# A 64-column bf16 product that nobody reads, in front of four weight blocks of every up stage and of the gated unit's output product

## The chip, the cores and the metric

The kernel runs on one core of a Trainium2 chip. The time is device microseconds of that core for one launch, from inputs in HBM to the output in HBM. The kernel before took 1655.77 us, the median of three runs (1654.12 to 1661.84). The profiled execution took 1660.22 us, of which 1658.4 us is the span from the first to the last instruction.

## The reference

Two blocks of transformer layers over one sequence of 256 tokens with model width 1024, all in float32. What matters here are the six feed-forward networks (two with a short convolution, four plain SwiGLU) and the gated unit (gMLP) between them; the two attention mixers and the linear recurrence lie around them.

```python
def conv_ffn(x, w_up, conv_w, conv_b, w_down):          # twice, D_FF = 2816
    h = x @ w_up                                        # (256,1024) @ (1024,5632)
    h = depthwise_causal_conv3(h, conv_w) + conv_b
    gate, up = split(h, 2)
    return (silu(gate) * up) @ w_down

def swiglu(n, w_gate, w_up, w_down):                    # four times
    return (silu(n @ w_gate) * (n @ w_up)) @ w_down

def gmlp_mixer(n, w_in, ln_g, ln_b, w_s, b_s, w_out):   # once
    u, v = split(gelu(n @ w_in), 2)
    sv = causal_mix_of_positions(w_s, layer_norm(v, ln_g, ln_b)) + b_s
    return (u * sv) @ w_out                             # (256,2048) @ (2048,1024)
```

Every network takes `rms_norm` of the running sum h, and its result is added to h (in the second block after another `rms_norm`).

## The kernel before, in words

All products run in float32 accuracy from three products of a faster float32 form: activations and weights are each split into a high part and a rest (hi, lo), and xh*wh, xl*wh and xh*wl are added up in PSUM. So TensorE does three products of 256 columns for each 128x128 tile of weights.

A weight block is 1024 rows by 256 columns (1 MB). `fetch` brings it from HBM by SyncE's DMA queue into one of three `wst` buffers; `unit` (L228) splits it: ScalarE writes `whi` (L249), VectorE writes `wlo` (L251), in four pieces for the first blocks of a stage and whole afterwards, into four buffers each. `feat2` (L267) then computes 256 output features for all 256 tokens: two halves of 24 products (`feat`, L261 to L265), 48 in all, into one of four PSUM buffers `acc`. `tok` (L280 to L291) is the same with the tokens as rows.

An up stage has 11 passes, i = 0 to 10, with two blocks each (gate and up columns). In `conv_ffn` (L663) every pass uses `feat2`. In `swiglu` (L626) passes 1 to 10 use `feat2`, and pass 0 does, in the last three of the four networks, something else (L635 to L653): the norm's factor comes late, so both blocks are computed token half by token half with `tok_turn`; ScalarE applies silu to each half (L645), VectorE multiplies (L646, result `ffu`), and TensorE turns `ffu` back to feature rows by four transposes (L650), two for each token half, into the PSUM buffer `turned`. Before them `p.finish()` (L647) broadcasts the factor with two products (L370); in the network beside which the shared keys are prepared it also transposes h for them, in four groups of four (L412), each into one of two PSUM buffers `mx`, which ScalarE and VectorE (L306, L308) must have emptied before.

After the 11 passes `down` (L545) multiplies the hidden features by the down weights (L565 to L567, and L576 to L578 for its last quarter or half), and at its quarters h is updated and transposed for the next norm (L400, L412).

I call the networks by their order: conv 1, conv 2, SwiGLU 1 to 4. SwiGLU 2 follows the gated unit; SwiGLU 3 carries the shared keys; SwiGLU 4 ends the program. SwiGLU 2, 3 and 4 have the special pass 0.

The order on each engine is fixed when the program is built: a scheduler runs through the program with a time model and lays down each engine's queue. It may let a product that is written later overtake an earlier one that is not ready. `behind()` (L192) forbids that: what is issued within it stands behind the instruction that was written last on TensorE. Each engine takes its queue strictly in order.

Of the kernel before, what the change touches and what calls it, by code (L numbers as in the profile page):

```python
# [15 lines left out]
P = 128  # L16
D = 1024
T = 256
KD = 8
# [35 lines left out]
MLA_ORDER = "N0 V0 N1 V1 V2 P0 P1 Q0 R0 Q1 R1 S0 Q2 S1 T0 Q3 O0 S2 T1 S3 V3 O1 T2 O2 T3 O3"  # L55
TURN_OLD, TURN_NEW = (8, 5), (6, 4)
N_HOLD = 3
N_START = 12
L_MLA = 2
RSQRT_BITS = float(0x5F375A86)  # L60
# [87 lines left out]
class Net:  # L148
# [48 lines left out]
    def warm(s, n):  # L197

        if n:
            with s.behind():  # L200
                ps = s.prod()
                x = s.ident.bitcast(BF16)
                for _ in range(n):
                    s.nc.tensor.matmul(ps[:, :T], x[:, :P], x, start=True, stop=True)


    def fetch(s, parts, k0, nk, cuts=1):

# [55 lines left out]
            mm(ps, wh[:, k, cols], xl, start=False, stop=False)  # L264
            mm(ps, wl[:, k, cols], xh, start=False, stop=k == nk - 1)  # L265

    def feat2(s, w, x, c=0, beside=None):  # L267

        ps = s.acc()
        s.parts(lambda j: s.feat(w, c + j, x, ps[:, j * T:(j + 1) * T]), beside)  # L270
        return ps

# [202 lines left out]
    def start(s, first):  # L475
# [29 lines left out]
        p = s.pre(s.vec("attn_norm"))  # L505
        s.warm(N_START)
        for n in range(4):
# [37 lines left out]
    def down(s, w, hid, kn, out, n_beside=0):  # L545
# [36 lines left out]
        for n in range(4 - out.late, 4):  # L582
            ps = [s.acc()[:, :T], s.acc()[:, :T]]
            for i, (k0, nk) in enumerate(spans):
                u = s.unit([(w, n * T, T)], k0, nk)
                for t in range(2):
                    if len(spans) - i > N_HOLD:
                        part(ps[t], t, u, k0)
# [37 lines left out]
    def swiglu(s, p, wg, wu, wd, out, beside=None):  # L626
        nc = s.nc
        hid = Split(s, "f", KF)
        s.begin(p)
        for i in range(KF // 2):  # L630
            if beside and i == 3:
                beside()
            g, u = s.e("ffg"), s.m("ffu")
            h2 = lambda x: x.rearrange("p (j t) -> p j t", j=2)
            if p.halves and i == 0:  # L635

                units = [s.unit([(m, 0, T)], 0, KD) for m in (wg, wu)]
                turned = s.mix()
                for t in range(2):
                    c, ps, r = slice(t * T, (t + 1) * T), s.acc(), p.r[:, t:t + 1]  # L640
                    s.tok_turn(p, units, t, ps, () if t else TURN_NEW)
                    if not t:
                        last = p.marks[-1][0]
                    with s.tc.issue_after(last):
                        nc.scalar.activation(g[:, c], ps[:, :T], AF.Silu, scale=r)  # L645
                    nc.vector.scalar_tensor_tensor(u[:, c], ps[:, T:], r, g[:, c], op0=OP.mult, op1=OP.mult)  # L646
                p.finish()  # L647
                for t in range(2):
                    for j in range(2):
                        nc.tensor.transpose(turned[:, j * T + t * P:j * T + (t + 1) * P],  # L650
                                            u[:, t * T + j * P:t * T + (j + 1) * P], s.ident)
                s.split(hid.hi.pair(0), hid.lo.pair(0), turned)
                continue  # L653
            ps = s.feat2(s.unit([(wg, i * T, T)], 0, KD), p.x)
            nc.vector.tensor_tensor(h2(g), h2(ps), s.rb2(p), op=OP.mult)
            nc.scalar.activation(g, g, AF.Silu)
            ps = s.feat2(s.unit([(wu, i * T, T)], 0, KD), p.x)
            nc.vector.tensor_tensor(h2(u), h2(ps), s.rb2(p), op=OP.mult)  # L658
            nc.vector.tensor_tensor(u, u, g, op=OP.mult)
            s.split(hid.hi.pair(i), hid.lo.pair(i), u)  # L660
        s.down(wd, hid, KF, out)

    def conv_ffn(s, p, l, out):  # L663
        nc, a = s.nc, s.a
        w = a["ffn_w_up"][l]
        hid = Split(s, "f", KF)
        s.begin(p)

        def conv(y, x, c):
            taps = [s.vec("conv_w%d%d" % (i, l), c, 1) for i in range(3)]  # L670
            nc.scalar.activation(y, x, AF.Identity, scale=taps[2], bias=s.vec("conv_b%d" % l, c, 1))
            nc.vector.scalar_tensor_tensor(y[:, 1:], x[:, :T - 1], taps[1], y[:, 1:], op0=OP.mult, op1=OP.add)
            nc.vector.scalar_tensor_tensor(y[:, 2:], x[:, :T - 2], taps[0], y[:, 2:], op0=OP.mult, op1=OP.add)

        h2 = lambda x: x.rearrange("p (j t) -> p j t", j=2)
        for i in range(KF // 2):
            if l == 0 and i in (3, 6):

                if i == 3:
                    turns = s.conv_vectors(1)  # L680
                else:
                    with s.behind():
                        for turn in turns:
                            turn()
            ys = [s.e("cvg"), s.m("cvu")]
            for y, first in zip(ys, (0, KF)):
                c = first + 2 * i
                ps = s.feat2(s.unit([(w, c * P, T)], 0, KD), p.x)
                x = s.z("cvx")
                nc.vector.tensor_tensor(h2(x), h2(ps), s.rb2(p), op=OP.mult)  # L690
                for j in range(2):
                    half = slice(j * T, (j + 1) * T)
                    conv(y[:, half], x[:, half], c + j)
                if not first:
                    nc.scalar.activation(y, y, AF.Silu)
            g, u = ys
            nc.vector.tensor_tensor(u, u, g, op=OP.mult)
            s.split(hid.hi.pair(i), hid.lo.pair(i), u)
        s.down(a["ffn_w_down"][l], hid, KF, out)
# [690 lines left out]
    def gmlp(s, p, out):  # L1390
        nc, a = s.nc, s.a
        V, S, PE = nc.vector, nc.scalar, nc.tensor
        w = a["gmlp_w_in_2"][0]
# [5 lines left out]
        for c in range(4):  # L1399
            units = [s.unit([(w, half + (2 * c + j) * T, T)], 0, KD) for j in range(2)]  # L1400
            for t in range(2):
# [7 lines left out]
                ps = s.acc()  # L1409
# [19 lines left out]
        for c in range(8):  # L1429
            ps = s.feat2(s.unit([(w, c * T, T)], 0, KD), p.x)  # L1430
            x, y = s.e("gx"), s.m("gy")
            V.tensor_tensor(h2(x), h2(ps), s.rb2(p), op=OP.mult)
            S.activation(x, x, AF.Gelu_apprx_tanh)
            sp = s.prod()
            for j in range(2):
                g = 2 * c + j
                cols = slice((g % 4) * P, (g % 4 + 1) * P)
                for n in range(2):
                    i = 2 * j + n
                    PE.matmul(sp[:, i * P:(i + 1) * P], v[n][g // 4][:, cols], wt[g // 4][:, cols],  # L1440
                              start=True, stop=True)
            for j in range(2):
                g = 2 * c + j
                cols = slice((g % 4) * P, (g % 4 + 1) * P)
                hf = slice(j * T, (j + 1) * T)
                V.scalar_tensor_tensor(h2(y[:, hf]), h2(sp[:, hf]), ln_g[:, g:g + 1],
                                       radd[g // 4][:, cols][:, None, :].to_broadcast([P, 2, P]),
                                       op0=OP.mult, op1=OP.add)
            V.tensor_tensor(y, y, x, op=OP.mult)
            s.split(z.hi.pair(c), z.lo.pair(c), y)  # L1450
        s.down(a["gmlp_w_out_2"][0], z, 16, out)

    def rope_tables(s):
# [322 lines left out]
```

## Time and profile before

| | |
|---|---|
| Median of three runs | 1655.77 us (1654.12 to 1661.84) |
| Profiled execution | 1660.22 us, span 1658.4 us |
| TensorE products (PE) | busy 1622.1 us, 98% of the span, 14500 of them |
| VectorE (DVE) | busy 1150.2 us, 69% |
| ScalarE (ACT) | busy 913.1 us, 55% |
| HBM | 291.19 MB read, 178 GB/s over the span |

A busy time is a union of intervals, and products overlap in it, so 98% does not say that TensorE runs as fast as it can: for that one counts products in a stretch. PEclk in the views is the granted TensorE clock, 1.00 being 2.4 GHz and 0.50 being 1.2 GHz. PEld is the loading of the weights of a product.

### The profile page before, as it was taken

The numbers are of one execution on the slowest core, as the hardware profiler recorded it, in microseconds if no ns is written. First come the engines' busy times: TensorE is split into PE (matmuls) and PEld (weight loads), VectorE is DVE, ScalarE is ACT, GpSimd is POOL, SyncE is SP. The second block draws the span as 40 slices with busy tenths as digits, with TensorE's granted clock in tenths as the row PEclk, the third lists the DMA queues.
The fourth block names the chain that finished last, engine by engine and source line by source line (L and its number), as shares of the span: only waits on it lengthen the run. The fifth ranks groups of instructions, "written<-read, shape, count | busy, mean of one in ns | idle before, by whom it ended". The sixth has DMA issues, their size and how long they took to land.

```text
span 1658.4 us, 34159 instructions
## 1 busy us (share of the span) xinstructions
PE 1622.1 (98%) x14500; PEld 1608.4 (97%) x14502; DVE 1150.2 (69%) x1900; ACT 913.1 (55%) x1443; POOL 6.7 (0%) x28
## 2 busy tenths in 40 slices
PE   8989999996999999999999999999999999999998
PEld 8979999995999999999999999999999999999998
DVE  6997899545769975766668757664676647576643
ACT  7876665443666555544466446444664448574442
POOL 0000000000000000000000000000000000000000
PEclk9999999997999999999999999999999999999999
DMA  8733655677546556556756556556475665446551
GB/s 266 220 97 114 200 178 188 191 141 177 157 149 208 173 181 216 182 186 217 231 161 211 168 175 197 186 169 206 130 233 189 193 201 151 132 153 212 189 190 58
DMA packets 303821, 297.58 MB, mean 179 GB/s; under 512 B 14295, under 2 KB 300214, under 8 KB 303670
## 3 DMA queue, kind: packets, MB, share of 16 engines
q1 hardware_dynamic: 303622, 295.40, 57.4%
q8 instruction: 114, 1.87, 0.5%
q14 instruction: 37, 0.30, 0.1%
q10 hardware_dynamic: 48, 0.01, 0.0%
HBM read 291.19 MB, written 4.19 MB: 178 GB/s over the span
## 4 chain that ended last, share of the span: by engine, by line
PE 88%; DVE 4%; DMA 3%; ACT 3%; issue 1%; SPq 0%; DVEq 0%; ACTq 0%
PE acc L263 16%; PE acc L265 16%; PE acc L264 16%; PE acc L565 8%; PE acc L567 7%; PE acc L566 7%; PE acc L289 2%; PE acc L290 2%; PE acc L291 2%; DMA bias_rows<-rrow 2%; PE acc L576 2%; PE acc L578 2%; PE acc L577 2%; DVE wlo L251 1%; ACT whi L249 1%
## 5 line engine op out<-in xcount | busy, mean ns | idle before, releaser
L249 ACT ACTIVATE whi<-wst 128x2048 fp32r<-128x2048 f32 (+4 forms) x404 | 523.8, 1330 | 517.5 <-issue 228.6
L251 DVE TENSOR_TENSOR wlo<-wst,whi 128x2048 fp32r<-128x2048 f32 (+4 forms) x404 | 621.0, 1561 | 251.6 <-ACT whi L249 249.6
L264 PE MATMUL acc<-xl,whi 128*128 128x256 f32 x2416 | 675.2, 280 | 1.1 <-DVE xl L308 1.1
L263 PE MATMUL acc<-xh,whi 128*128 128x256 f32 x2416 | 675.3, 281 | 0.8 <-ACT xh L306 0.4
L265 PE MATMUL acc<-xh,wlo 128*128 128x256 f32 x2416 | 674.7, 280 | 0.5 <-DVE wlo L251 0.5
L264 PEld LDWEIGHTS acc<-xl,whi 128*128 128x128 f32 x2416 | 458.1, 190 | 1.7 <-DVE xl L308 1.5
L265 PEld LDWEIGHTS acc<-xh,wlo 128*128 128x128 f32 x2416 | 455.0, 189 | 0.9 <-DVE wlo L251 0.7
L263 PEld LDWEIGHTS acc<-xh,whi 128*128 128x128 f32 x2416 | 454.3, 188 | 1.6 <-ACT xh L306 0.7
L567 PE MATMUL acc<-wlo,fh 128*128 128x256 f32 x880 | 245.3, 279 | 0.0
L565 PE MATMUL acc<-whi,fh 128*128 128x256 f32 x880 | 244.7, 279 | 0.0
L566 PE MATMUL acc<-whi,fl 128*128 128x256 f32 x880 | 244.5, 278 | 0.0
L567 PEld LDWEIGHTS acc<-wlo,fh 128*128 128x128 f32 x880 | 165.2, 188 | 0.0
L565 PEld LDWEIGHTS acc<-whi,fh 128*128 128x128 f32 x880 | 165.0, 188 | 0.0
L566 PEld LDWEIGHTS acc<-whi,fl 128*128 128x128 f32 x880 | 164.9, 187 | 0.0
L289 PE MATMUL acc<-whi,xh 128*128 128x256 f32 x384 | 108.9, 284 | 0.0
L291 PE MATMUL acc<-wlo,xh 128*128 128x256 f32 x384 | 106.8, 278 | 0.0
L290 PE MATMUL acc<-whi,xl 128*128 128x256 f32 x384 | 106.8, 278 | 0.0
L289 PEld LDWEIGHTS acc<-whi,xh 128*128 128x128 f32 x384 | 72.1, 188 | 0.2
L290 PEld LDWEIGHTS acc<-whi,xl 128*128 128x128 f32 x384 | 72.1, 188 | 0.0
L291 PEld LDWEIGHTS acc<-wlo,xh 128*128 128x128 f32 x384 | 72.1, 188 | 0.0
L658 DVE TENSOR_TENSOR ffu<-acc,rb 128x512 f32<-128x512 f32 x41 | 28.3, 691 | 48.5 <-PE acc L265 48.3
L308 DVE SCALAR_TENSOR_TENSOR xl<-mx,vectors,xh 128x128 fp32r<-128x128 f32 (+1 forms) x124 | 39.1, 376 | 23.1 <-ACT xh L306 23.0
(422 smaller groups left out, 2097.3 us busy)
## 6 DMA issues: line engine op xcount, KB each, us to landing
wst<-in_ffn_w_up_dram SPq DMA_DIRECT2D x88, 1024.0 KB, 5.2
wst<-in_ffn_w_down_dram SPq DMA_DIRECT2D x48, 1024.0 KB, 5.9
wst<-in_ffn_w_gate_dram SPq DMA_DIRECT2D x44, 1024.0 KB, 5.4
wst<-in_ffn_w_down_dram SPq DMA_DIRECT2D x24, 768.0 KB, 4.8
wst<-in_gmlp_w_in_dram SPq DMA_DIRECT2D x16, 1024.0 KB, 5.4
wst<-in_hgrn_w_in_dram SPq DMA_DIRECT2D x13, 1024.0 KB, 5.5
wst<-in_gmlp_w_out_dram SPq DMA_DIRECT2D x8, 1024.0 KB
wst<-in_dsa_w_in_dram SPq DMA_DIRECT2D x6, 1024.0 KB
```

Source lines behind the costliest of these rows:

```text
L249: s.nc.scalar.activation(hi[:, c], w[:, c], AF.Copy)
L251: s.nc.vector.tensor_tensor(lo[:, c], w[:, c], hi[:, c].bitcast(F32), op=OP.subtract)
L263: mm(ps, wh[:, k, cols], xh, start=k == 0, stop=False)
L264: mm(ps, wh[:, k, cols], xl, start=False, stop=False)
L265: mm(ps, wl[:, k, cols], xh, start=False, stop=k == nk - 1)
L289: mm(ps, xh[:, ts], wk, start=k == 0, stop=False)
L290: mm(ps, xl[:, ts], wk, start=False, stop=False)
L291: mm(ps, xh[:, ts], lk, start=False, stop=k == nk - 1)
L308: b = s.nc.vector.scalar_tensor_tensor(lo, src, g, hi.bitcast(F32), op0=OP.mult, op1=OP.subtract)
L565: mm(ps[t], xh, wh[:, k], start=k0 + k == 0 and not both, stop=False)
L566: mm(ps[t], xl, wh[:, k], start=False, stop=False)
L567: mm(ps[t], xh, wl[:, k], start=False, stop=k0 + k == kn - 1 and (t == 1 or not both))
```

## The change

`pace` issues one product of the bf16 identity matrix with 64 of its own columns into a `pr` buffer in PSUM, behind whatever was written before it. Nobody reads the result. With `paced=True`, `feat2` issues such a product first, puts the first half of its 24 products behind it, and then the second half. It is on for passes i = 1 and i = 2 of all six up stages, two blocks each, and one `pace` stands in front of the gated unit's `down`: 25 products in all.

```diff
+PACED = (1, 2)
...
+    def pace(s):
+
+        with s.behind():
+            s.nc.tensor.matmul(s.prod()[:, :64], s.identb, s.identb[:, :64], start=True, stop=True)
...
-    def feat2(s, w, x, c=0, beside=None):
+    def feat2(s, w, x, c=0, beside=None, paced=False):

         ps = s.acc()
+        if paced:
+            s.pace()
+            with s.behind():
+                s.feat(w, c, x, ps[:, :T])
+            s.feat(w, c + 1, x, ps[:, T:])
+            return ps
         s.parts(lambda j: s.feat(w, c + j, x, ps[:, j * T:(j + 1) * T]), beside)
         return ps
...
-            ps = s.feat2(s.unit([(wg, i * T, T)], 0, KD), p.x)
+            ps = s.feat2(s.unit([(wg, i * T, T)], 0, KD), p.x, paced=i in PACED)
             nc.vector.tensor_tensor(h2(g), h2(ps), s.rb2(p), op=OP.mult)
             nc.scalar.activation(g, g, AF.Silu)
-            ps = s.feat2(s.unit([(wu, i * T, T)], 0, KD), p.x)
+            ps = s.feat2(s.unit([(wu, i * T, T)], 0, KD), p.x, paced=i in PACED)
...
-                ps = s.feat2(s.unit([(w, c * P, T)], 0, KD), p.x)
+                ps = s.feat2(s.unit([(w, c * P, T)], 0, KD), p.x, paced=i in PACED)
...
+        s.pace()
         s.down(a["gmlp_w_out_2"][0], z, 16, out)
```

The line numbers move by up to 14: L263 to L265 become L270 to L272, L289 to L291 become L302 to L304, L370 becomes L383, L412 becomes L425, L650 becomes L663; the new product is L211.

The queue of TensorE at the end of pass 0 of SwiGLU 2, before (L291 ends pass 0, `ffu` is the turned input of L650, `pr` the factor's broadcast, L263 begins pass 1):

```order
L291 MATMUL acc<-wlo,xh 128x256
L650 MATMUL mx<-cst,ffu 128x128 x2
L370 MATMUL pr<-cst,pr 128x128
L263 MATMUL acc<-xh,whi 128x256
...
L650 MATMUL mx<-cst,ffu 128x128 x2
L264 MATMUL acc<-xl,whi 128x256
```

The second pair of transposes stands 70 products behind the start of pass 1. The same place now:

```order
L304 MATMUL acc<-wlo,xh 128x256
L663 MATMUL mx<-cst,ffu 128x128 x2
L383 MATMUL pr<-cst,pr 128x128
L663 MATMUL mx<-cst,ffu 128x128 x2
L211 LDWEIGHTS identb
L211 MATMUL pr<-identb 128x64
L270 MATMUL acc<-xh,whi 128x256
```

Both pairs now stand in front of the new product and so in front of all of pass 1; in SwiGLU 4 the rows move in the same way, by 70 products.

The queue of TensorE at the same place of SwiGLU 3, before (L412 are the groups of transposes of h for the shared keys):

```order
L291 MATMUL acc<-wlo,xh 128x256
L370 MATMUL pr<-cst,pr 128x128
L412 MATMUL mx<-cst,h 128x128 x4
L263 MATMUL acc<-xh,whi 128x256
...
L412 MATMUL mx<-cst,h 128x128 x4
...
L412 MATMUL mx<-cst,h 128x128 x4
...
L650 MATMUL mx<-cst,ffu 128x128 x4
```

The second group stands 14 products, the third 79 and the four transposes of `ffu` 84 products behind the start of pass 1. Now:

```order
L304 MATMUL acc<-wlo,xh 128x256
L383 MATMUL pr<-cst,pr 128x128
L425 MATMUL mx<-cst,h 128x128 x12
L663 MATMUL mx<-cst,ffu 128x128 x4
L211 LDWEIGHTS identb
L211 MATMUL pr<-identb 128x64
L270 MATMUL acc<-xh,whi 128x256
```

All three groups and the four transposes stand in front of pass 1.

## Rows read from the trace of the kernel before

**Rows 1.** The page: busy time by engine, and the chain that ended last.

```profile
PE 1622.1 (98%) x14500; PEld 1608.4 (97%) x14502; DVE 1150.2 (69%) x1900; ACT 913.1 (55%) x1443; POOL 6.7 (0%) x28
...
PE 88%; DVE 4%; DMA 3%; ACT 3%; issue 1%; SPq 0%; DVEq 0%; ACTq 0%
```

**Rows 2.** Windows, PE: stretch, length, busy (products), clock, DMA share, GB/s.

```profile
172.40:228.80 56.40, 56.40 (x481) 1.00 0.59 188
485.00:618.50 133.50, 133.50 (x1136) 1.00 0.58 188
947.20:988.80 41.60, 41.60 (x356) 1.00 0.62 197
1017.00:1178.00 161.00, 161.00 (x1370) 1.00 0.61 194
1487.40:1650.00 162.60, 162.60 (x1383) 1.00 0.53 170
679.00:839.00 160.00, 160.00 (x1414) 1.00 0.67 213
1236.40:1372.80 136.40, 136.40 (x1206) 1.00 0.60 190
```

**Rows 3.** Timeline, PE, two interruptions: start, us, instruction.

```profile
132.85 0.38 PE L1026 MATMUL acc<-cst,zero 128*128 128x512 bf16 x1 [0.16 <-issue]
...
133.19 0.28 PE L1018 MATMUL acc<-whi,zl 128*128 128x256 f32 x1
...
228.84 0.28 PE L265 MATMUL acc<-xh,wlo 128*128 128x256 f32 x1
228.97 0.38 PE L466 MATMUL mx<-cst,vst 128*128 128x128 f32 x2
...
229.30 0.28 PE L264 MATMUL acc<-xl,whi 128*128 128x256 f32 x1
```

**Rows 4.** Timeline, end of pass 0 of SwiGLU 2: PE, ACT, DVE.

```profile
1005.76 0.37 PE L263 MATMUL acc<-xh,whi 128*128 128x256 f32 x1
...
1013.80 0.38 PE L650 MATMUL mx<-cst,ffu 128*128 128x128 f32 x2
...
1003.67 6.07 ACT L249 ACTIVATE whi<-wst 128x512 fp32r<-128x512 f32 x9
1009.65 0.45 ACT L645 ACTIVATE ffg<-acc,pr 128x256 f32<-128x256 f32 x1
...
1011.99 0.48 DVE L646 SCALAR_TENSOR_TENSOR ffu<-acc,pr,ffg 128x256 f32<-128x256 f32 x1
```

**Rows 5.** Timeline, the same place of SwiGLU 4: PE, DVE.

```profile
1476.10 0.37 PE L263 MATMUL acc<-xh,whi 128*128 128x256 f32 x1
...
1482.32 0.48 DVE L646 SCALAR_TENSOR_TENSOR ffu<-acc,pr,ffg 128x256 f32<-128x256 f32 x1
```

**Rows 6.** Timeline, the same place of SwiGLU 3: PE, DVE.

```profile
1195.34 0.37 PE L263 MATMUL acc<-xh,whi 128*128 128x256 f32 x1
...
1202.06 2.15 DVE L308 SCALAR_TENSOR_TENSOR xl<-mx,vectors,xh 128x128 fp32r<-128x128 f32 x8
```

**Rows 7.** Timeline, PE, its longest wait.

```profile
372.60 0.28 PE L263 MATMUL acc<-xh,whi 128*128 128x256 f32 x1
389.04 0.58 PE L1109 MATMUL pr<-dki,dqi 128*128 128x128 f32 x1 [16.17 <-ACT drl L1112]
```

**Rows 8.** Windows, PE, around that wait and at the end; PEclk follows the busy time.

```profile
376.00:378.00 2.00, 0.00 (x0) 0.76 0.89 101
389.00:394.00 5.00, 4.96 (x23) 0.50 1.10 343
...
1645.00:1658.00 13.00, 6.53 (x56) 0.83 0.24 81
```

**Rows 9.** Timeline, the factor of conv 1: DVE writes it, PE broadcasts it.

```profile
168.92 0.16 DVE L342 SCALAR_TENSOR_TENSOR rc<-rs_u,rs_y 128x2 f32<-128x2 f32 x1
...
171.04 0.60 PE L370 MATMUL pr<-cst,rc 128*128 128x128 f32 x4
```

## The prediction, made before the changed kernel ran

> **What bounds the kernel now.** Read the page first: TensorE is busy 98% of the span and makes up 88% of the chain that ended last [rows 1]. So whatever adds a slot to TensorE's queue adds to the time, and so does whatever makes it wait. Then count products in long undisturbed stretches, since busy time hides their spacing [rows 2]. Each count takes in some two products that only reach in at the edges, so I take off two. In conv 2 that gives 133.5 us / 1134 = 117.7 ns a product; SwiGLU 2 161.0 / 1368 = 117.7; SwiGLU 4 162.6 / 1381 = 117.7; conv 1 (first half of its up stage) and the gated output product the same (56.4 / 479 and 41.6 / 354). But SwiGLU 1 has 160.0 / 1412 = 113.3 ns, and SwiGLU 3 136.4 / 1204 = 113.3, with the same products at the same full clock. So the stream has two spacings, a wide one of 117.7 and a tight one of 113.3 ns, each of which holds for more than a thousand products, and which one a stage gets is settled where other instructions come in between. That is the only thing which an unread product could improve. Last come the places where the queue moves: there the reader is to compare when TensorE starts pass 1 with when the inputs of the moved transposes are ready [rows 4 to 6].
>
> **The change part by part.** The sum starts from the profiled execution, 1660.2 us.
>
> *25 new products.* Two nearby interruptions are in the trace [rows 3]. The two records of L466 stretch the distance from L265 to L264 to 0.46 us where it would be 0.235 (two slots of 117.7), so 0.11 us a record. A bf16 product of 512 columns is followed 0.34 us later by the second product behind it, 0.22 more than one slot. A product with 64 columns lies between 0.03 us (an eighth of that 0.22) and 0.11. A transpose of 128 columns costs a whole slot though it has half the columns, so I take the upper end: 25 x 0.11 = 2.8 us; the lower is 0.7. Nothing hides it, as TensorE is the bound.
>
> *The transposes of SwiGLU 2 and 4 now stand in front of pass 1.* The second pair needs the second half of `ffu`. In SwiGLU 2 ScalarE works off nine split pieces from 1003.67 before it gets to silu at 1009.65, VectorE has its own share of them to do, and `ffu` is ready at 1011.99 + 0.48 = 1012.47 [rows 4]. Before, this cost nothing: the pair stood at 1013.80, behind 70 products. TensorE was free for pass 1 at 1005.76. In the built program ScalarE's and VectorE's queues stand in the same order up to that point, and the splits do not wait for TensorE there, so `ffu` comes no earlier. TensorE then waits 1012.47 - 1005.76 = 6.7 us, with all of pass 1 behind the pair. In SwiGLU 4 it is 1482.32 + 0.48 - 1476.10 = 6.7 us [rows 5]. Later the queue has no wait that could give this back.
>
> *SwiGLU 3.* The third group of transposes for the keys needs a `mx` buffer which VectorE empties in the run of L308 that ends at 1202.06 + 2.15 = 1204.21, and `turned` needs the next one, free at its end; pass 1 can start after four transposes more, at about 1204.7 instead of 1195.34 [rows 6]. Of these 9.3 us, 12 x 0.11 = 1.3 us is transposing that was done later before. So 8.0 us. The three waits make 21.4 us; their bounds, if ScalarE's and VectorE's pieces come half a microsecond earlier or later in each, are 20 and 23.
>
> *The clock after these waits.* In its longest wait TensorE's last product started at 372.60, the next at 389.04 [rows 7]; the window 376 to 378 with a mean of 0.76 says that the clock went from 2.4 to 1.2 GHz at about 377.0, 4.2 us after that product ended. At the end of the program the last 13 us have 6.53 us of products and a mean of 0.83, so it fell 4.4 us before 1658, at 1653.6, 2.1 us after the last product. Idle times of 6.7 us and more are longer than both, so I expect the fall in all three. After the long wait the clock was still low for about five microseconds of work: 23 products in 5 us, 0.217 us apart [rows 8], so 23 x 0.1 = 2.3 us lost. Three times: 6.9 us; the lower bound is nothing.
>
> *The broadcast of conv 1* (L370) stands 21 products earlier now, at about 171.04 - 2.47 = 168.6, while its factor is ready at 169.08 [rows 9]: 0.5 us. In conv 2 it moves 14 products and stays covered by them.
>
> *The spacing.* The streams at 117.7 ns which run undisturbed from a paced block on count 479 + 1134 + 354 + 1368 + 1381 = 4716 products [rows 2]. All of them at 113.3 gives back 4716 x 4.4 ns = 20.8 us. In the other direction the 1412 + 1204 products at the tight spacing can go to the wide one: 11.5 us more. No row shows what a product like the new one does to the spacing; but conv 2 is wide and SwiGLU 1 behind it tight, SwiGLU 2 wide and SwiGLU 3 tight, so interruptions change it in both directions. I take the upper end, 20.8, on an argument: the tight stream is even, and a unit always has 48 products, so every one of the paces meets it at the same point; if it survives one it survives all, and four in a row give a wide stream four chances. This is the weakest step.
>
> Here a rule of the Trainium skill speaks against the gain. "TensorE: Matmul & The Clock Gate", section "Step-by-step: what each phase is for", has TensorE read moving columns and weights over two independent ports, so that loading the next weights takes nothing from the running product; there would be one spacing and nothing to win, and the sum would be the one of "costs only" below. The windows with 117.7 and 113.3 ns at the same clock do not agree with one spacing.
>
> Sum: 1660.2 + 2.8 + 21.4 + 6.9 + 0.5 - 20.8 = 1671.0 us. The timed median lies 4.4 us under the profiled execution; the three runs differ by 7.7 us, about what one SwiGLU stage gains by its spacing (1381 x 4.4 ns = 6.1 us), so the mixture of spacings probably differs from run to run. With all streams tight that mixture no longer matters, and I take off only 1: 1670 us.
>
> **The rivals.** *Half of it*: some streams stay wide and one of the tight ones is lost, 10 us gained on balance: 1681 us. For it: the conv 1 stream is disturbed again at 228.97 and SwiGLU 3 by the keys' products after its paces. *Costs only*: spacings fall as they did, 1691.8 us. For it: conv 1 meets L466 in its middle [rows 3], SwiGLU 4 the transposes, and both run wide all the same; an interruption need not change anything. *All wide*: the new product always leaves the wide spacing, 1691.8 + 11.5 = 1703 us; for it: five of the seven windows are wide; against it, that two are not. *Not slower*: the paces also make streams tight that come after later interruptions (the rest of conv 1 and the ends of the down products, some 150 us or 1280 products, 5.6 us more), and the clock does not fall in the waits: 1660.2 + 2.8 + 21.4 + 0.5 - 26.4 = 1658.5 us. It decides from the point where the tight streams gain more than the 24.7 us of waits and slots, 5600 products; against it, rows 8. Were moreover one of the three waits not to arise, it would be 1651. That the change does not do what it says is possible only for the spacing, and is "costs only".
>
> **How the numbers follow.** The forecast (most or all paced streams tight, the waits paid) 0.45, its own range 1663 to 1677; half of it 0.20; costs only 0.17; all wide 0.09; not slower 0.09. A measurement of this kernel can tell about 0.5% from no change, that is 1647.5 to 1664.1. Faster gets 0.06 (the best part of "not slower", and a wait misread), the same 0.14 (the rest of it and the lower edge of the forecast), slower 0.80. The range leaves out a tenth at each end: 1657 to 1697.
>
> **What would show it.** The first product of pass 1 in SwiGLU 2, 3 and 4 comes some 7 to 9 us after the last one of pass 0, its wait named after VectorE (`ffu`, and in SwiGLU 3 `xl`), and the clock reads 0.50 for some 5 us there. Windows in conv 2, SwiGLU 2 and SwiGLU 4 count 113.3 ns a product from the second paced pass on. The new product takes one slot. If pass 1 starts without a wait, the step on the transposes is wrong and the kernel is faster; if windows still show 117.7, it is the step on the spacing.

## The result, and the profile after

The changed kernel took **1675.62 us**, the median of four runs (1674.80 to 1676.31), against 1654.94 us of the kernel before beside it (four runs, 1652.66 to 1661.84): ratio 1.0136, 95% interval 1.0101 to 1.0170. It is slower by 1.4%, and the interval lies clear of 1. The forecast was 1670 us, with a range of its own from 1663 to 1677. The profiled execution took 1676.31 us, span 1674.4 us, which is 16.0 us more than the 1658.4 us of before.

The page after, block 1 and the chain, against [rows 1]:

```profile
PE 1616.7 (97%) x14527; PEld 1599.7 (96%) x14527; DVE 1152.2 (69%) x1900; ACT 912.6 (55%) x1443; POOL 6.7 (0%) x28
...
PE 89%; ACT 5%; DVE 3%; DMA 2%; issue 1%; SPq 0%; DVEq 0%; ACTq 0%
```

There are 27 more records of products, 25 of them new (the second profile of the kernel before, in e5 below, has 14502 records, so the other two were missing in the first), and yet TensorE is busy 5.4 us less in a longer span. So products became cheaper and waits were added. The waits of TensorE after (us in total, times, the longest):

```profile
PE pr L1122 <- ACT drl L1125: 16.1, 1, 16.1
PE mx L663 <- DVE ffu L659: 12.5, 2, 6.2
PE mx L425 <- DVE xl L321: 6.8, 1, 6.8
...
PE acc L271 <- DVE xl L321: 2.3, 5, 0.5
...
PE acc L270 <- ACT xh L319: 1.1, 2, 0.8
```

The first was there before (16.2 us the longest). The next two lines, 19.3 us, are new: the transposes of `ffu` in SwiGLU 2 and 4, and the third group for the keys in SwiGLU 3. The last two are small waits of products for their inputs, 3.4 us together; for the same two lines the view of before lists 1.5.

**The spacing.** Windows of TensorE after, in conv 1, conv 2, SwiGLU 1, the gated output, SwiGLU 2, 3 and 4 (stretch, length, busy and products, clock, DMA share, GB/s), against [rows 2]:

```profile
178.00:228.00 50.00, 50.00 (x443) 1.00 0.61 198
507.00:615.00 108.00, 108.00 (x955) 1.00 0.59 194
692.00:838.00 146.00, 146.00 (x1290) 1.00 0.67 212
948.00:988.00 40.00, 40.00 (x355) 1.00 0.63 200
1032.00:1180.00 148.00, 148.00 (x1308) 1.00 0.61 195
1250.00:1385.00 135.00, 135.00 (x1193) 1.00 0.60 192
1515.00:1665.00 150.00, 150.00 (x1325) 1.00 0.52 168
```

Taking off two products each, all seven are tight: 113.3 or 113.4 ns a product (conv 2 108 us / 953, SwiGLU 2 148 / 1306, SwiGLU 4 150 / 1323). Before, five of them were wide, at 117.7.

**The wait in SwiGLU 2.** Timeline after, around the end of pass 0, against [rows 4]:

```profile
1005.20 0.39 PE L383 MATMUL pr<-cst,pr 128*128 128x128 f32 x2
...
1011.29 0.48 DVE L659 SCALAR_TENSOR_TENSOR ffu<-acc,pr,ffg 128x256 f32<-128x256 f32 x1
...
1011.83 0.69 PE L663 MATMUL mx<-cst,ffu 128*128 128x128 f32 x2 [6.24 <-DVE ffu L659]
...
1012.31 0.26 PE L211 MATMUL pr<-identb 128*128 128x64 bf16 x1
```

TensorE ends pass 0 with the factor's broadcast at 1005.2, the transposes wait until `ffu` is there at 1011.77 (1011.29 + 0.48), and the first new product follows, with all of pass 1 behind it. The clock there, in the same stage and then in SwiGLU 4:

```profile
1010.00:1012.00 2.00, 0.17 (x1) 0.50 1.09 360
1012.00:1014.00 2.00, 2.00 (x10) 0.50 1.09 348
1014.00:1016.00 2.00, 2.00 (x12) 0.50 1.09 348
1016.00:1018.00 2.00, 2.00 (x18) 0.94 0.72 187
...
1496.00:1498.00 2.00, 2.00 (x11) 0.50 1.09 349
...
1500.00:1502.00 2.00, 2.00 (x16) 0.77 0.79 204
```

The clock goes to 1.2 GHz in the wait and stays there for some 4 us of work in SwiGLU 2 and 6 in SwiGLU 4: 10 to 12 products in 2 us instead of 17 or 18.

**SwiGLU 3**, timeline after, against [rows 6]:

```profile
1204.42 2.15 DVE L321 SCALAR_TENSOR_TENSOR xl<-mx,vectors,xh 128x128 fp32r<-128x128 f32 x8
...
1205.59 1.12 PE L425 MATMUL mx<-cst,h 128*128 128x128 f32 x4 [6.85 <-DVE xl L321]
...
1207.53 0.26 PE L211 MATMUL pr<-identb 128*128 128x64 bf16 x1
```

The third group of the keys' transposes waits 6.85 us for the buffer that L321 empties, as the prediction had it.

**What was not foreseen: the entry of conv 1.** Timeline after, at the end of pass 0:

```profile
168.74 0.51 PE L270 MATMUL acc<-xh,whi 128*128 128x256 f32 x2 [0.80 <-ACT xh L319]
...
169.75 0.39 PE L271 MATMUL acc<-xl,whi 128*128 128x256 f32 x1 [0.50 <-DVE xl L321]
...
173.16 0.60 PE L383 MATMUL pr<-cst,rc 128*128 128x128 f32 x4
```

The last products of pass 0 wait for the last groups of x. Before, TensorE had no wait that the profile lists between 150 and 180 us. Nor is the broadcast (L383) late: its factor is ready at 170.81, and it starts at 173.16, one slot behind the product in front of it.

**And one piece that is not of the change:** for some 3.4 us around 110 us, in the recurrence in front of conv 1 and of every new product, the clock was low in this execution:

```profile
108.00:110.00 2.00, 2.00 (x15) 0.57 0.00 0
```

Five other traces (e6, e7, e9, e10 and e12) have such a fall at the same place, and in the eight others, both of the kernel before among them, the clock is 1.00 there. What decides it is not shown.

**Where the 16 us come from.** Matching each product of after with the same product of before gives by how much it starts later (us of the two traces):

| product at | before | after | later by | since the row above |
|---|---|---|---|---|
| in front of conv 1 | 154.5 | 156.3 | 1.8 | 1.8, of which 1.5 with the low clock at 108 |
| conv 1, pass 2 | 184.7 | 189.2 | 4.5 | 2.7, entry with three new products |
| conv 1, up behind L466 | 245.0 | 248.0 | 3.0 | -1.5, tight until 229 |
| conv 2, pass 1 | 479.5 | 484.3 | 4.7 | 0.5 in conv 1's down, 1.2 at the entry, no new product yet |
| conv 2, end of up and most of down | 615.2 | 615.3 | 0.1 | -4.6, tight |
| SwiGLU 1 | 690.5 | 691.4 | 0.9 | 0.8, of which four new products |
| end of the gated output | 991.8 | 991.3 | -0.5 | -1.4, tight |
| SwiGLU 2, pass 1 | 1021.9 | 1030.2 | 8.3 | 8.8, wait, clock, three new products |
| SwiGLU 2, end | 1187.7 | 1190.1 | 2.4 | -5.9, tight |
| SwiGLU 3, behind pass 2 | 1217.8 | 1230.5 | 12.7 | 10.3, wait, clock, four new products |
| end of SwiGLU 4's pass 0 | 1474.3 | 1486.7 | 12.4 | -0.3 |
| SwiGLU 4, pass 1 | 1489.3 | 1511.2 | 21.9 | 9.5, wait, clock, three new products |
| end of the program | 1658.4 | 1674.4 | 16.0 | -5.9, tight |

### The profile page after: what moved, and what is told of

Its sections match the earlier page's. It is cut to its first block, busy times and chain, and to the rows that moved or that the text cites. A ratio compares the mean times of both kernels' runs of the same rounds, so it can differ in the third digit from the quotient of the medians.

```text
span 1674.4 us, 34208 instructions
## 1 busy us (share of the span) xinstructions
PE 1616.7 (97%) x14527; PEld 1599.7 (96%) x14527; DVE 1152.2 (69%) x1900; ACT 912.6 (55%) x1443; POOL 6.7 (0%) x28
## 4 chain that ended last, share of the span: by engine, by line
PE 89%; ACT 5%; DVE 3%; DMA 2%; issue 1%; SPq 0%; DVEq 0%; ACTq 0%
PE acc L270 17%; PE acc L271 17%; PE acc L272 17%; PE acc L578 7%; PE acc L580 7%; PE acc L579 7%; ACT whi L256 2%; PE acc L302 2%; DMA wst<-in_dsa_w_in_dram 2%; PE acc L304 2%; PE acc L303 2%; PE acc L591 1%; PE acc L589 1%; PE acc L590 1%; DVE wlo L258 1%
## 5 line engine op out<-in xcount | busy, mean ns | idle before, releaser
L270 PE MATMUL acc<-xh,whi 128*128 128x256 f32 x2416 | 676.5, 281 | 1.6 <-ACT xh L319 1.1
L272 PE MATMUL acc<-xh,wlo 128*128 128x256 f32 x2416 | 672.9, 279 | 0.4 <-DVE wlo L258 0.4
L270 PEld LDWEIGHTS acc<-xh,whi 128*128 128x128 f32 x2416 | 457.4, 190 | 2.8 <-ACT xh L319 1.8
L272 PEld LDWEIGHTS acc<-xh,wlo 128*128 128x128 f32 x2416 | 458.6, 190 | 0.8 <-DVE wlo L258 0.6
L580 PE MATMUL acc<-wlo,fh 128*128 128x256 f32 x880 | 245.0, 278 | 0.0
L302 PE MATMUL acc<-whi,xh 128*128 128x256 f32 x384 | 108.9, 284 | 0.0
L304 PE MATMUL acc<-wlo,xh 128*128 128x256 f32 x384 | 106.9, 278 | 0.0
L302 PEld LDWEIGHTS acc<-whi,xh 128*128 128x128 f32 x384 | 72.1, 188 | 0.2
L304 PEld LDWEIGHTS acc<-wlo,xh 128*128 128x128 f32 x384 | 72.1, 188 | 0.0
L668 DVE TENSOR_TENSOR ffg<-acc,rb 128x512 f32<-128x512 f32 x41 | 28.3, 691 | 37.9 <-PE acc L272 26.0
```

Source lines behind the costliest of these rows:

```text
L270: mm(ps, wh[:, k, cols], xh, start=k == 0, stop=False)
L302: mm(ps, xh[:, ts], wk, start=k == 0, stop=False)
L304: mm(ps, xh[:, ts], lk, start=False, stop=k == nk - 1)
L580: mm(ps[t], xh, wl[:, k], start=False, stop=k0 + k == kn - 1 and (t == 1 or not both))
```

## The experiments

**The theory:** the new product sets the tight spacing and is worth some 20 us; the order that comes with it (`behind()` in pass 1) makes TensorE wait and costs some 30. **The rivals:** the order or the standstill sets the spacing; the products are themselves the cost; each product is only a chance.

The table shows what spacing the streams had in each kernel: windows 515:605, 700:825, 1040:1160, 1260:1355 and 1520:1620 us of its profile, 766 or 767, 1063 or 1064, 1021 or 1022, 809, and 851 products at the wide spacing (W), 796 or 797, 1105 or 1106, 1061 or 1062, 840 or 841, and 884 or 885 at the tight one (T); no other counts occur.

| kernel | conv 2 | SwiGLU 1 | SwiGLU 2 | SwiGLU 3 | SwiGLU 4 | median us | ratio to before (95%) |
|---|---|---|---|---|---|---|---|
| before | W | T | W | T | W | 1654.9 | |
| before, again (e5) | W | T | W | T | T | 1651.4 | 0.9985 (0.9964 to 1.0006) |
| changed | T | T | T | T | T | 1675.6 | 1.0136 (1.0101 to 1.0170) |
| order only (e1) | W | W | T | T | W | 1688.1 | 1.0236 (1.0188 to 1.0284) |
| in pass 2 only, 13 (e2) | T | T | T | T | T | 1643.1 | 0.9955 (0.9935 to 0.9975) |
| one for each stage, 7 (e3) | T | T | T | T | T | 1640.5 | 0.9940 (0.9915 to 0.9965) |
| changed, waits filled (e4) | T | T | T | T | T | 1670.5 | 1.0118 (1.0081 to 1.0154) |
| 7, with 256 columns (e6) | W | W | W | W | W | 1671.3 | 1.0106 (1.0072 to 1.0140) |
| 7, with 128 columns (e9) | W | W | W | W | W | 1669.6 | 1.0109 (1.0073 to 1.0146) |
| 7, float32 form, 64 columns (e7) | W | T | W | T | T | 1650.6 | 0.9977 (0.9953 to 1.0000) |
| 7, float32 transposes (e11) | T | W | T | T | T | 1646.7, one run | |
| 7 and 21 more (e8) | T | T | T | T | T | 1641.9 | 0.9930 (0.9903 to 0.9957) |
| 7 and 8 in down products (e10) | T | T | T | T | T | 1642.5, one run | |
| 7, in mid-block (e12) | T | T | T | T | T | 1641.6 | 0.9932 (0.9915 to 0.9950) |

The gated output, which the table leaves out, held 257 or 258 products in 952:982 us (wide) in the kernel before, e5, e1 and e7, and 264 to 268 (tight) in all the others.

The kernel before had medians of 1650 to 1655 us beside these, in runs from 1643.6 to 1662.5. The sets of runs were taken on different chips, so a kernel is compared by its ratio to the kernel before beside it.

**e1, the order without the product.**

```diff
         if paced:
-            s.pace()
             with s.behind():
...
-        s.pace()
         s.down(a["gmlp_w_out_2"][0], z, 16, out)
```

> The changed kernel without its 25 unread products; the order that they brought (each half block behind what was written before it) stays. Theory (the product sets the tight spacing, the order makes the waits): conv 2, the gated output, SwiGLU 2 and SwiGLU 4 run at 117.7 ns again as before, the waits in front of pass 1 of SwiGLU 2, 3 and 4 stay at 6 to 7 us each with the clock at 0.50, so the time is that of before plus the losses that the two traces show at the same instructions (2.5 us at the entry of conv 1, 1 of conv 2, 8, 10.5 and 9 in SwiGLU 2, 3 and 4): 1655 + 31 = 1686 us. Rival A (the order or the standstill in front of pass 1 sets the spacing, the product nothing): tight spacing without the product, about 1672. Rival B (the unread products are what costs): without them 1650 to 1658.

Measured 1688.1 us. The waits of TensorE, and the windows of SwiGLU 1, 2 and 4:

```profile
PE mx L663 <- DVE ffu L659: 12.5, 2, 6.2
PE mx L425 <- DVE xl L321: 7.1, 2, 6.8
```

```profile
700.00:825.00 125.00, 125.00 (x1064) 1.00 0.65 204
1040.00:1160.00 120.00, 120.00 (x1061) 1.00 0.62 197
1520.00:1620.00 100.00, 100.00 (x851) 1.00 0.57 181
```

The waits are all there without a single new product, the small ones at the entry of conv 1 too (0.8 and 1.0 us there). Matched with the kernel before as in the result's table, the order alone puts the products behind the start of pass 1 later by 8.7, 9.9 and 8.4 us in SwiGLU 2, 3 and 4. So the order costs, and the product pays back. The spacing is not as expected in detail: SwiGLU 2 came out tight and SwiGLU 1 wide. So a changed order changes spacings too, in both directions; without the 64-column product no kernel here has all five tight. Rival A, by which the order alone gives the tight spacing, falls with conv 2 and SwiGLU 4.

**e2, only in pass 2.**

```diff
-PACED = (1, 2)
+PACED = (2,)
```

> Unread products only in front of the two blocks of pass 2 (and of the gated unit's output product), 13 instead of 25; in pass 1 the queue of TensorE is that of before, so the late transposes and the products that fill the entry of conv 1 and conv 2 stand where they stood. Theory: no wait in front of pass 1, no fall of the clock there, tight spacing from pass 2 on: 20.3 us gained in the changed kernel less 4 streams x 96 products x 4.4 ns = 1.7 us, 13 products cost 13 x 0.11 = 1.4: 1655 - 18.6 + 1.4 = 1638 us. Rival A (any product of the kind brings the waits, wherever it stands): 1670 to 1676. Rival B (it is the standstill or the products in pass 1 that settle the spacing; pass 2 comes too late): 1655 to 1657.

Measured 1643.1 us. None of the three waits is left, nor those at the entries of conv 1 and conv 2, and all five streams are tight. That is the theory's case, at 5 us more than it said. Part of it is in the profiled execution: behind the long wait for the gathered keys TensorE waited 3.06 us a second time for the same line (0.30 us in the first profile of before), and then the clock was at 0.57 from 396 to 400 us. Part is that the kernel before was itself under 1655 here (1650.1). Rivals A and B fall.

**e3, one product for each stage.** From here on every version but e4 and e5 has these edits, and the later fences leave them out.

```diff
-PACED = (1, 2)
+PACED = (2,)
...
-            ps = s.feat2(s.unit([(wu, i * T, T)], 0, KD), p.x, paced=i in PACED)
+            ps = s.feat2(s.unit([(wu, i * T, T)], 0, KD), p.x)
...
-                ps = s.feat2(s.unit([(w, c * P, T)], 0, KD), p.x, paced=i in PACED)
+                ps = s.feat2(s.unit([(w, c * P, T)], 0, KD), p.x, paced=i in PACED and not first)
```

> One unread product for each up stage, in front of the first block of pass 2 (and one in front of the gated unit's output product): 7 in all. Theory (one product leaves the tight spacing whatever was there, and it stays until something else comes in between): every stream that is tight with 13 products is tight with 7, 6 x 0.11 = 0.7 us less than with 13: about 1637 us. Rival (each product is only a chance, four or two are needed): one or two of conv 1, conv 2, SwiGLU 2 and SwiGLU 4 stay at 117.7 ns, each 2 to 6 us: 1641 to 1650.

Measured 1640.5 us, all streams tight, and the other 18 products of the change buy nothing more. But only conv 1 and conv 2 were wide where their product stood; there one product was enough. The four SwiGLU streams came in tight already: in SwiGLU 2 the last 19 steps in front of the product take 2.15 us, 113 ns each. SwiGLU 2 came in tight in e2, e3, e8, e10, e11 and e12 and wide in both profiles of before, e6, e7 and e9; what decides that is not shown, so its 5.9 us can't be put down to the product in e2 and e3. Conv 2's product stood in a wide stream and left a tight one; timeline around it, with the middle of the run left out:

```profile
491.84 0.28 PE L272 MATMUL acc<-xh,wlo 128*128 128x256 f32 x1
491.96 0.20 PE L211 MATMUL pr<-identb 128*128 128x64 bf16 x1
492.00 0.36 PE L270 MATMUL acc<-xh,whi 128*128 128x256 f32 x1
492.20 0.28 PE L271 MATMUL acc<-xl,whi 128*128 128x256 f32 x1
...
493.23 0.28 PE L271 MATMUL acc<-xl,whi 128*128 128x256 f32 x1
...
493.91 0.28 PE L271 MATMUL acc<-xl,whi 128*128 128x256 f32 x1
```

In front, 0.12 us from product to product; 0.04 from the new one to the next and 0.20 to the one after; and then 6 products in 0.68 us, 113.3 ns each.

**e4, the waits filled with unread products.**

```diff
                 for t in range(2):
+                    if t and not beside:
+                        s.warm(54)
                     for j in range(2):
                         nc.tensor.transpose(turned[...
```

> The changed kernel, and between the two pairs of transposes of ffu in SwiGLU 2 and SwiGLU 4 stand 54 unread bf16 products of 256 columns each, some 6 us of work for TensorE in the 6.5 us in which it waits. The wait for ffu stays, only the standstill goes. Theory (a part of the loss is the clock that falls in the wait and comes back late: 4.2 us of work at half clock in SwiGLU 2, 5.9 in SwiGLU 4): the clock stays at 1.00 there and half of that comes back, 5 us: 1676 - 5 = 1671 us. Rival A (the clock's fall costs nothing, the transposes wait anyway): 1676. Rival B (filling is late itself, or ScalarE and VectorE come later beside it): over 1677.

Measured 1670.5 us (1669.1 to 1670.9), 5.1 under the changed kernel. The windows in SwiGLU 2 and 4 behind the waits:

```profile
1012.00:1016.00 4.00, 4.00 (x37) 1.00 1.08 325
...
1494.00:1498.00 4.00, 4.00 (x38) 1.00 0.95 280
```

The clock stays at 2.4 GHz, and 37 products fit where 22 did. Matched product by product with the changed kernel, 2.2 us come back in SwiGLU 2 and 2.8 in SwiGLU 4. So the fall of the clock cost 5 us in these two places, apart from the waits.

**e5, the kernel before again,** with no edit.

> The kernel before, unchanged, for a second profile of it. Theory (without the product the spacing of a stream is left to chance and may differ from run to run, which is why the runs of the kernel before lie 1643.6 to 1662.5 us, 19 us apart, and those of the kernels with products 1638 to 1647): in this profile at least one of the long streams (conv 1, conv 2, SwiGLU 1 to 4, the gated output) has another spacing than in the first profile, and the difference of the two times is that of the products at 113.3 ns times 4.4 ns. Rival (the order of the program fixes each spacing, and the runs differ by waits, such as that for the gathered keys): conv 2, SwiGLU 2 and SwiGLU 4 at 117.7 and SwiGLU 1 and 3 at 113.3 ns again.

Measured 1651.4 us; span of its profile 1650.8, against 1658.4. Windows in conv 1 behind L466, and in SwiGLU 4:

```profile
235.00:280.00 45.00, 45.00 (x400) 1.00 0.56 183
1520.00:1620.00 100.00, 100.00 (x885) 1.00 0.59 192
```

In the first profile the same stretches held 385 and 851 products: here both are tight. 1381 products of SwiGLU 4 at 4.4 ns are 6.1 us of the 7.6. So chance is part of it, as the theory said; but conv 2, SwiGLU 1, 2 and 3 were the same in both, so the program's order has a say too, as the rival had it. The two profiles may be of two chips; but the 23 runs of before beside e1 to e4 are all of one chip and lie 19 us apart, so the chip alone does not explain the spread.

**e6 and e9, the same product with more columns.**

```diff
-            s.nc.tensor.matmul(s.prod()[:, :64], s.identb, s.identb[:, :64], start=True, stop=True)
+            s.nc.tensor.matmul(s.prod()[:, :256], s.identb, s.cst.bitcast(BF16)[:, :256], start=True, stop=True)
```

> One unread product for each up stage, as in the kernel with 7 products, but with 256 columns instead of 64 (bf16 as there). Theory A (a bf16 product with its own weight load sets the tight spacing, whatever its columns): conv 1, conv 2, SwiGLU 2, SwiGLU 4 and the gated output tight behind it, time that of 7 products plus 7 x 0.08 us: 1641. Theory B (it is the short product, which leaves a gap for the next weight load): 256 columns leave the spacing as it was, wide in some of the five, 1645 to 1655.

Measured 1671.3 us: the five streams of the table and conv 1 in front of L466 wide, also SwiGLU 1 and 3, which were tight in both profiles of before. Neither theory said that: in the up stages the product does not leave the spacing alone, it sets the wide one. The gated output is the exception, and theory A had that one right. Its window before, and here:

```profile
952.00:982.00 30.00, 30.00 (x257) 1.00 0.66 214
...
952.00:982.00 30.00, 30.00 (x267) 1.00 0.60 201
```

There the same product stands behind small products of another kind and in front of down products, and it left the tight spacing. With 128 columns:

> One unread bf16 product for each up stage with 128 columns (64 left each of the streams tight, 256 left each wide). Theory (what counts is how long the product itself runs beside the next weight load): with 128 columns either all streams behind it are tight, time as with 64, 1640 to 1642, or all are wide, time as with 256, 1669 to 1672. Rival (the two results differ for another reason, and each stream falls by itself): a mixture, as in the kernel before, 1645 to 1660.

Measured 1669.6 us, again the table's five wide and the gated output tight. Timeline at its product in SwiGLU 4:

```profile
1496.57 0.28 PE L272 MATMUL acc<-xh,wlo 128*128 128x256 f32 x1
1496.68 0.23 PE L211 MATMUL pr<-identb 128*128 128x128 bf16 x1
1496.72 0.36 PE L270 MATMUL acc<-xh,whi 128*128 128x256 f32 x1
1496.92 0.28 PE L271 MATMUL acc<-xl,whi 128*128 128x256 f32 x1
...
1498.10 0.28 PE L272 MATMUL acc<-xh,wlo 128*128 128x256 f32 x1
...
1499.16 0.28 PE L272 MATMUL acc<-xh,wlo 128*128 128x256 f32 x1
```

The steps around it are the same, 0.04 and 0.20 us, and yet behind it nine products take 1.06 us, 117.8 ns each. One up stream stepped out of line, conv 1, which came in wide and was tight behind the 128 columns.

**e7, 64 columns in the float32 form of the stream.**

```diff
+        identr = s.cp.tile([P, P], F32R, name="identr")
+        nc.vector.tensor_copy(identr, s.ident)
...
-            s.nc.tensor.matmul(s.prod()[:, :64], s.identb, s.identb[:, :64], start=True, stop=True)
+            s.nc.tensor.matmul(s.prod()[:, :64], s.identr, s.identr[:, :64], start=True, stop=True)
```

> One unread product for each up stage with 64 columns, but in the float32 form of the stream instead of bf16 (its weights the identity in that form). Theory A (the bf16 weight load, shorter than that of the stream, sets the tight spacing): the stream keeps the spacing that it had, wide in some of conv 1, conv 2, SwiGLU 2, SwiGLU 4 and the gated output: 1645 to 1655. Theory B (any short product does it): all five tight, about 1640.

Measured 1650.6 us. All six up streams kept behind it what they had in front, four tight and two wide. Theory A as far as it goes: a short product in the stream's own form changes nothing here, the bf16 one does. That the shorter weight load is the reason is not shown.

**e11, one transpose in plain float32.**

```diff
-            s.nc.tensor.matmul(s.prod()[:, :64], s.identb, s.identb[:, :64], start=True, stop=True)
+            s.nc.tensor.transpose(s.prod()[:, :P], s.ident, s.ident)
```

> One unread transpose of 128 columns in plain float32 for each up stage instead of the bf16 product. Theory (only the bf16 product sets the spacing; a single float32 transpose leaves it as it was, as the lone transpose of the vectors in the middle of conv 1 does): each stream keeps behind it what it had in front. Rival (it takes a slot of its own kind and always leaves the one or the other): the same spacing behind all six.

Both missed: conv 1 and conv 2 went from wide to tight, SwiGLU 1 and 3 from tight to wide (SwiGLU 3 came back behind the keys' products), SwiGLU 2 and 4 stayed tight. So the bf16 product is not the only one that changes a spacing, and what this one leaves differs from place to place.

**e8, 21 more products.** Behind each group of transposes of the down products' `residual`, of the recurrence's output, and behind each lone transpose:

```diff
+        if pace:
+            s.pace()
         last = s.split_scaled([(*p.x(2 * n + j), ps[:, j * T:(j + 1) * T], p.gain[:, 2 * n + j:2 * n + j + 1])
...
             nc.tensor.transpose(ps[:, :P], st, s.ident)
+            if hasattr(s, "identb"):
+                s.pace()
```

> The kernel with 7 products, and 21 more: one behind every group of transposes in the down products of conv 1, conv 2 and the mixers before them, and behind each lone transpose of the vectors. Theory (streams stay wide behind such transposes until a product of the kind comes): the streams at 22 to 69, 132 to 163, 303 to 346 and 611 to 653 us of the trace with 7 products, some 1200 products, go from 117.7 to 113.3 ns: 5.3 us gained, 21 x 0.12 = 2.5 us paid: 1640.5 - 2.8 = 1638 us. Rival (groups of about 100 products between two interruptions are too short, or the products disturb the order there): 1640 to 1645.

Measured 1641.9 us, no better than with 7: the rival. Of the eight groups of transposes behind the quarters of conv 1 and conv 2, four had a wide stream behind the product and four a tight one; directly behind these transposes it does not settle the spacing. Two of the four tight ones stand in front of up products of the next network, all four wide ones in front of down products.

**e10, in the down products, behind products of the stream.**

```diff
                     mm(ps[t], xh, wl[:, k], start=False, stop=k0 + k == kn - 1 and (t == 1 or not both))
+                    if n and not out.late and not both and k0 + k == 2 and t:
+                        s.pace()
```

> The kernel with 7 products, and one more in the second to fourth quarter of the down products of conv 1, conv 2 and the second mixer, after some 20 products of the quarter. In the third and fourth quarter of conv 1 and conv 2 it stands 7 products of the stream behind the last group of transposes (in the version with 21 more products it stood directly behind the transposes and most streams stayed wide); in the second quarter the transposes come after it. Theory (the product sets the tight spacing when a product of the stream stands in front of it): the third and fourth quarters of conv 1 and conv 2, 4 x 90 products, at 113.3 ns, the second wide; 1.6 us gained, 8 x 0.12 = 1 us paid, no difference in the time. Rival (down products, which load the split weights as the other operand, do not take the tight spacing from it): 117.7 ns in all quarters.

Measured 1642.5 us, one run, no difference in the time; but the theory missed its streams. At the first of them, in conv 1, the stream came in tight and left wide:

```profile
300.48 0.28 PE L580 MATMUL acc<-wlo,fh 128*128 128x256 f32 x1
...
301.05 0.39 PE L580 MATMUL acc<-wlo,fh 128*128 128x256 f32 x2
301.28 0.20 PE L211 MATMUL pr<-identb 128*128 128x64 bf16 x1
301.31 0.36 PE L578 MATMUL acc<-whi,fh 128*128 128x256 f32 x1
301.52 0.28 PE L579 MATMUL acc<-whi,fl 128*128 128x256 f32 x1
...
302.58 0.28 PE L579 MATMUL acc<-whi,fl 128*128 128x256 f32 x1
```

In front 5 products in 0.57 us; behind, 9 in 1.06. All six quarters of conv 1 and conv 2 were wide behind it, and both of the second mixer.

**e12, in mid-block of the up stages.**

```diff
+            if k == pace:
+                s.pace()
...
-            s.pace()
             with s.behind():
-                s.feat(w, c, x, ps[:, :T])
+                s.feat(w, c, x, ps[:, :T], pace=3)
```

> The kernel with 7 products, but in the up stages the product stands 12 products later: in the middle of a half block, between products of one accumulation, as it stood in the down products, where it left 117.7 ns in all six quarters of conv 1 and conv 2. Theory (its place counts: only in front of a block does it set the tight spacing): 117.7 ns behind all six, 1665 to 1672 us. Rival (the kind of stage counts, up products take the tight spacing from it anywhere): 113.3 ns behind all six, 1640 to 1642.

Measured 1641.6 us, all six up streams tight behind it. Only conv 2 came in wide here, and its product made it tight. So it is not the place within a block: the theory falls, the rival holds as far as conv 1 and conv 2 go. The same product left the tight spacing among up products and the wide one in the down products of those two networks; the down products of the gated output, tight behind it, say that the kind of stage is not all of it.

## Why the prediction was right, and where it was not

**The verdict and its mechanism** held: tight streams pay for less than the waits cost. Its sum was 10.8 us over the profiled execution of before; measured are 16.0.

**The spacing**, called the weakest step, was right in effect: -20.8 foretold, -19.3 by the table (1.5 + 4.6 + 1.4 + 5.9 + 5.9). The argument behind it, that four in a row give four chances, was not needed: in the seven kernels with 64 bf16 columns all 16 products that met a wide up stream at full clock made it tight, each by itself. No row had shown that, and with 128 columns it would have been wrong in five of six up stages (e9), so that the term came out is in part luck. It is also measured against a first profile in which SwiGLU 4 was wide; in the second one it is tight without any product, and SwiGLU 4 of the changed kernel came back tight behind its wait, in front of its second product (its first ran at 1.2 GHz). "Costs only" and "half of it" fall with the windows; the case "costs only" would have been about e1's 1688.

**The three waits and the clock** were foretold at 21.4 + 6.9 us, with the ten new products that the three rows of the table hold 29.4; by the table it is 8.8 + 10.3 + 9.5 = 28.6. The rows of before gave the start of pass 1 in each of the three to within 0.6 us: `ffu` was ready when it had been ready, and TensorE no earlier. Of the clock's 6.9, two thirds (4.6) belong to SwiGLU 2 and 4; e4 measured 5.1.

**The failing term is the entry of the conv networks:** 0.5 us for the broadcast of conv 1, and conv 2 "stays covered". Measured are 2.7 us with three new products (some 0.4 us) and 1.2 us without any; the waits listed there are 1.8 and 0.7 us. The broadcast was never late. What was missed is that `behind()` in pass 1 also takes away the filling: before, products of pass 1 could overtake the last products of pass 0 while these had to wait for the last groups of x; now nothing may. e1 has the same waits without a product, e2 and e3 list none there. The prediction looked at what stands behind the moved transposes, and not at what had stood in front of the waits that it took for nothing.

**The new product** took a little more than the 0.11 us foretold: in a tight stream the steps around it are 118, 38, 202, 119, 116 and 114 ns where five slots would be 567, so 0.14 us, 3.5 us for the 25 instead of 2.8. And some 1.5 us are the low clock at 108 us, which no term of the sum could hold.

**The rival on the other side** ("not slower") needed more tight streams than waits; e2 and e3 show that it was the waits that had to go. "All wide" was no idle case either: 64 columns more would nearly have brought it (e9).

## What to carry to other kernels

Ask of an inserted instruction not only what it does but what its ordering forbids: the kernel loses 1.4% with the product in passes 1 and 2, where in pass 1 other work used to overtake, and gains 0.6% with one product in pass 2. And where a long stream of products has two spacings from run to run, count products in windows before and after: busy time hides it, and one cheap instruction may settle it, in either direction.

## What the runs showed that was not expected

- A stream of these products at full clock holds one of two spacings, 113.3 or 117.7 ns, for over a thousand products; no window of the table shows anything between. Every bf16 product of 64 columns that ran at full clock among up products left the tight one (16 came in wide and the rest tight; at 1.2 GHz, in SwiGLU 2 and 3 of the changed kernel, it did not: the stream came back wide there, and the second product made it tight); with 256 columns the wide one in all six up stages, with 128 in five of six; 64 columns in the float32 form left it as it was (six of six). In the down products of conv 1 and conv 2 the 64 columns, behind products of the stream, left the wide one (six of six). In the gated output the bf16 product with 64, 128 and 256 columns and the float32 transpose all left the tight one. What in TensorE decides this was not found; the steps right at the product, 38 and 201 ns, are alike for 64, 128 and 256 columns.
- The same program takes one or the other in some streams from run to run: SwiGLU 4 and half of conv 1 differ in the two profiles of before, 7.6 us apart. So part of the spread of the kernel before, 19 us in these runs, is a spread of spacings; the runs of e2, e3, e8 and e12 lie within 2 to 8 us each.
- Best were e3 and e12 with 7 products and e8 with 28, 0.6 to 0.7% under the kernel before; they cannot be told apart.
